# Attention's second key group one chunk pair earlier in the filler, three filler steps ahead of the first scores, one gate unit fetched at a fixed place

## The chip, the core and the metric

One Trainium2 core of one chip. A launch works on one sequence of 1024 positions (1040 with 16 meta tokens). The metric is device time in microseconds (us), median of several runs, lower is better. A profile is one further execution, recorded by the hardware profiler. Its engines are TensorE (PE, with its weight loads as PEld), VectorE (DVE), ScalarE (ACT), GpSimd (POOL) and SyncE (SP), which here only starts transfers. Each engine takes its instructions in the order of its own stream; what follows a waiting instruction waits with it.

## What is computed

Cut to what matters. `u` is the normalised input of 1040 rows and 1024 columns; one projection `w_in` feeds everything.

```python
z = u @ w_in
rq, rk, rv, rg, aq, ak, av, ag, gr, ga = _split_in(z)
# branch A: 4 heads of retention, forward and backward scans over 9 chunks of 128
o_r = _bidirectional_retention(rq, rk, rv, lg_f, lg_b)
o_r = groupnorm(o_r) * silu(rg);  y_r = o_r @ w_rb
# branch B: 8 query heads in 2 key groups, window of 128 to both sides, 16 meta keys, a sink
s_band = einsum(qb, kb) * scale;  s_meta = einsum(qb, km) * scale
m = maximum(max(s), sink);  p = exp(s - m)
p = p / (sum(p) + exp(sink - m))
o_a = p_band @ vb + p_meta @ vm
o_a = o_a * silu(ag);  y_a = o_a @ w_ab
mix = sigmoid(gr) * y_r + sigmoid(ga) * y_a
return h + rms_norm(mix @ w_o, post_w)
```

aq and ak get rotary positions. Inputs and output are float32.

## The kernel before

**Arithmetic.** Each float32 operand is split into a high and a low part of a shorter type. The high part is a cast (on ACT, or on POOL in `pool_hi`, L86), the low part the difference (`dve_lo`, L89, always on DVE). A product is three matmuls, high by high (L73), low by high (L74), high by low (L75), in `mm3` (L70 to L76). Names end in `h` and `l` for the two parts, so `aqh` and `aql` are the parts of the rotated query `aq`.

**Stages.** First the four retention heads, h = 0 to 3, in `retention`. Each runs forward over nine chunks (`stage1` makes the values `vh`, `vl`, the decayed keys and the scores, `stage2` the state) and then backward over chunks 8 to 1, where `pb` is the product of the query with the backward state (L601), DVE adds it into the chunk's output `op` (L602), and DVE splits the next state into `Shb`, `Slb`. Then the attention values (`gen_av`, tiles `pav`). Then attention: 32 chunks (hp, n), hp = 0 to 3 a pair of query heads, n = 0 to 7 a block of 128 positions. hp 0 and 1 use key group 0, hp 2 and 3 key group 1. Behind it come the four dense phases z, r, a and o (gates, two branch projections, the output projection), with seven products in place of eight for each pair of 2 x 2 blocks.

**One attention chunk.** `stage1(hp, n)`: for each of the two heads three score matmuls `ps`, DVE's masked minimum into `raw` (L1336), ACT's exponential into `p` with its sum in `den` (L1339); then DVE's reciprocal (L1342) and POOL's division (L1349). `stage2`: PE transposes `p` into `pt` (L1359, L1362, L1366), ACT and DVE split the result into `pah`, `pal`, `pm`, `pbh`, `pbl`. `stage3`: ten matmuls with the values into `po`. The driver loop at the end of `attention` puts, for chunk k: `stage1` of k+1, `stage2` of k, a number of filler steps, `stage3` of k-1. The tables `FILL[hp][n]` give the number of filler steps.

**Filler.** Attention alone would leave PE waiting for the softmax, so other matmul work is cut into steps, which generators hand out one at a time: `gen_aq(hp, i, es)` projects queries (tile `paq`, eight steps of three matmuls of 512 columns for each head and half of the positions, then `rope_evac` rotates the result on DVE and POOL), `gen_ak(g, pieces)` projects the keys of group g (tile `pak`, eight steps of three matmuls of 256 columns for each quarter), and `pre` makes two of the four column blocks of some gate units ahead (tiles `pe`; `pre_fetch` loads the unit's weights from memory into two buffers of the tag `wr`, `pre_sums` combines them in three DVE subtractions and additions, `pre_parts` splits the result). After each step the list `BEGUN` names what else is issued there: splitting of weights (`half_w`), of queries (`split_q`, `aqh` on ACT L646, `aql` on DVE), of a key quarter (`keys(g, i)`: `kTh` on ACT L692, `kTl` on DVE), fetches and sums for gate units, and rows of sums of the input (`sum_fetch`, `sum_row`). These are issued behind the last exponential, reciprocal and splits that were issued before them.

**What each engine's order follows from.** The order within an engine is the order of issue in the program, moved by a list scheduler; `tc.issue_after(x)` and `follow(...)` keep a block behind named instructions. In head 3 of retention the filler is `gen_ak(0)`, eight steps of `pre` (gate unit 6) and `gen_aq(0, 0)`; unit 6 is fetched and summed in `gen_pre` when its first step is reached in the program; nothing holds these sums, and the scheduler has moved them forward on DVE, to the seam between head 2's backward and head 3's forward loop. `raw` is one tile for each of the two heads of a pair, allocated at n = 0 of each pair in a pool that lies over memory of the retention stage, so a first writer waits for what read that memory, here the store of retention outputs (`ost`).

The functions below are those of the kernel before, with the line numbers of its profile; lines of the changed kernel lie 6 to 14 higher.

## Time and profile before

| | us |
|---|---|
| median of 3 runs | 1087.58 |
| lowest and highest of them | 1086.63, 1088.8 |
| the profiled execution, its own time | 1089.63 |
| its span in the profile | 1087.8 |
| PE busy | 1060.5 |
| DVE busy | 880.7 |
| ACT busy | 510.3 |
| POOL busy | 201.8 |

The profile gives the busy time of each engine over the span. A row of its timeline reads: start, duration, engine, line, operation, output and input tiles, and in brackets how long the engine had been idle before and what released it. A row of a window reads: the stretch, its length, busy time and count of PE, PEld, DVE, ACT and POOL, then the clock that PE was granted (1.00 is full speed), the share of the transfer engines and GB/s. Median of the runs and profiled execution differ by 1089.63 - 1087.58 = 2.05 us.

### The profile page before, as it was taken

Reading aid. Unit: us, or ns where it says so; the run is one execution under the profiler, and the core shown is the slowest. Engines: PE = TensorE matmul, PEld = TensorE weight load, DVE = VectorE, ACT = ScalarE, POOL = GpSimd, SP = SyncE. Lnnn points to the kernel's source line nnn. Section 1 sums busy time; section 2 is a strip of 40 time slices with the busy share of each in tenths; the row PEclk is TensorE's granted clock in tenths of the full one; section 3 lists DMA queues with packets and bytes.
Section 4 is the critical chain, followed back from the end, with each engine's and each line's share of the span. In section 5 each row is a group of like instructions: output and inputs, shape, how many; then the busy total and the mean of one; then the engine's idle time right before and its main releaser. Section 6 shows DMA issues by size and latency. Waiting matters only on the chain.

```text
span 1087.8 us, 17211 instructions
## 1 busy us (share of the span) xinstructions
PE 1060.5 (97%) x5939; PEld 915.7 (84%) x5939; DVE 880.7 (81%) x1805; ACT 510.3 (47%) x1126; POOL 201.8 (19%) x268
## 2 busy tenths in 40 slices
PE   8999999999999999989999999999999999999997
PEld 7898999988988788978888888887888888787886
DVE  7897778868976687787977988999789899767765
ACT  7241432512513465665567655545556546333442
POOL 3334225243332222332210000000000000110032
PEclk9999999999999999998999999999999999999999
DMA  7121102113121145342447788899944656789464
GB/s 289 39 69 58 47 34 69 58 49 98 50 78 59 49 147 170 120 155 88 164 143 241 263 263 289 269 345 346 377 164 146 218 198 206 231 204 331 121 116 79
DMA packets 88152, 175.19 MB, mean 161 GB/s; under 512 B 8912, under 2 KB 30928, under 8 KB 87248
## 3 DMA queue, kind: packets, MB, share of 16 engines
q1 hardware_dynamic: 84176, 167.51, 45.7%
q0 software_dynamic: 3456, 6.29, 4.0%
q8 instruction: 47, 0.77, 0.3%
q14 instruction: 41, 0.34, 0.1%
q10 hardware_dynamic: 432, 0.28, 0.1%
HBM read 119.52 MB, written 57.67 MB: 163 GB/s over the span
## 4 chain that ended last, share of the span: by engine, by line
PE 85%; DVE 6%; DMA 3%; issue 2%; ACT 2%; POOL 1%; SPq 0%; DVEq 0%; ACTq 0%; POOLq 0%
PE bz L73 8%; PE bz L74 8%; PE bz L75 8%; PE pv L73 3%; PE pv L74 2%; PE pv L75 2%; PE br L74 2%; PE br L73 2%; PE br L75 2%; PE bo L74 2%; PE bo L73 2%; PE bo L75 2%; PE ba L74 2%; PE ba L73 2%; PE ba L75 2%
## 5 line engine op out<-in xcount | busy, mean ns | idle before, releaser
L1196 POOL DMA_DIRECT2D mx_d<-c1a x4 | 3.7, 917 | 402.6 <-DVE c1a L1187 402.6
L74 PE MATMUL bz<-T,llz 128*128 128x512 f32 x192 | 75.7, 394 | 0.0
L75 PE MATMUL bz<-T,lhz 128*128 128x512 f32 x192 | 75.6, 395 | 0.0
L73 PE MATMUL bz<-T,lhz 128*128 128x512 f32 x192 | 75.2, 394 | 0.0
L73 PE MATMUL pv<-wh,big 128*128 128x256 f32 x256 | 73.2, 286 | 1.2 <-DVE m_qk L185 1.2
L74 PE MATMUL pv<-wh,big 128*128 128x256 f32 x256 | 73.0, 285 | 0.0
L75 PE MATMUL pv<-wl,big 128*128 128x256 f32 x256 | 72.7, 284 | 0.0
L73 PE MATMUL bz<-big,lhz 128*128 128x512 f32 x176 | 69.0, 395 | 0.8 <-ACT lhz L895 0.8
L74 PE MATMUL bz<-big,llz 128*128 128x512 f32 x176 | 69.7, 396 | 0.0
L75 PE MATMUL bz<-big,lhz 128*128 128x512 f32 x176 | 69.3, 394 | 0.0
L1339 ACT ACTIVATE p<-raw,nm 128x401 f32<-128x401 f32 (+1 forms) x64 | 38.4, 601 | 39.9 <-DVE nm L1336 39.7
L73 PE MATMUL paq<-big,wh 128*128 128x512 f32 x128 | 52.6, 411 | 0.0
L74 PE MATMUL paq<-big,wl 128*128 128x512 f32 x128 | 51.2, 400 | 0.0
L1349 POOL TENSOR_SCALAR p<-p,den 128x400 f32<-128x400 f32 (+1 forms) x60 | 33.8, 576 | 93.5 <-DVE den L1342 86.2
L75 PE MATMUL paq<-big,wh 128*128 128x512 f32 x128 | 50.8, 397 | 0.0
L73 PEld LDWEIGHTS pv<-wh,big 128*128 128x128 f32 x256 | 48.2, 188 | 1.7 <-DVE m_qk L185 1.5
L74 PEld LDWEIGHTS pv<-wh,big 128*128 128x128 f32 x256 | 48.2, 188 | 0.2
L75 PEld LDWEIGHTS pv<-wl,big 128*128 128x128 f32 x256 | 48.3, 189 | 0.0
L74 PEld LDWEIGHTS bz<-T,llz 128*128 128x128 f32 x192 | 36.2, 188 | 8.4
L75 PEld LDWEIGHTS bz<-T,lhz 128*128 128x128 f32 x192 | 36.2, 188 | 8.4
L73 PEld LDWEIGHTS bz<-T,lhz 128*128 128x128 f32 x192 | 36.2, 188 | 8.4
L1336 DVE CUSTOM_DVE_ANT_0 raw<-ps,mask,nsink 128x400 f32<-128x400 f32 (+1 forms) x64 | 36.6, 598 | 6.0 <-PE ps L75 5.5
(630 smaller groups left out, 3633.6 us busy)
## 6 DMA issues: line engine op xcount, KB each, us to landing
wrz<-in_w_in_dram SPq DMA_DIRECT2D x32, 512.0 KB, 6.2
wr<-in_w_in_dram SPq DMA_DIRECT2D x29, 512.0 KB, 3.9
e<-e SPq DMA_DIRECT2D x40, 256.0 KB, 4.2
we<-in_w_in_dram SPq DMA_DIRECT2D x16, 512.0 KB, 4.0
tg<-tg_d SPq DMA_DIRECT2D x32, 256.0 KB, 4.9
T<-preT SPq DMA_DIRECT2D x6, 1024.0 KB, 8.0
oTr_d<-ost SPq DMA_DIRECT2D x16, 256.0 KB, 2.1
xs<-in_xT_dram SPq DMA_DIRECT2D x16, 256.0 KB, 2.9
```

Source lines behind the costliest of these rows:

```text
L73: nc.tensor.matmul(o, ah, bh, start=first, stop=False, **kw)
L74: nc.tensor.matmul(o, al, bh, start=False, stop=False, **kw)
L75: latest[:] = [nc.tensor.matmul(o, ah, bl, start=False, stop=last, **kw).ins]
L1196: nc.gpsimd.dma_start(d, to, accum_op=ALU.add)
L1336: nc.vector.tensor_tensor_reduce(raw[e_][:, 1:1 + wid], s[:, 0:wid], mask[:, mo:mo + wid], -SCALE, nsink[:, hd:hd + 1], ALU.add, ALU.min, ...
L1339: last["exp"] = nc.scalar.activation(p[:, 0:1 + wid], raw[e_][:, 0:1 + wid], AF.Exp, scale=-1.0, bias=nm_[:, e_:e_ + 1], accum_out=den[:, ...
L1349: nc.gpsimd.tensor_scalar(pt[e_][:, 0:wid], pt[e_][:, 0:wid], den[:, e_:e_ + 1], 1.0, op0=ALU.mult, op1=ALU.mult)
```

## The change

It moves work and adds none: every matmul, split, load and store of before is there, in another order. Three places:

- **Head 3 of retention.** The loads of the key weights and of gate unit 6 are called at the forward loop's chunk 1, and the three sums of unit 6 at chunk 2, behind that chunk's latest `vl`. `gen_pre` leaves both out where they have been made.
- **Start of attention.** The two `raw` tiles are allocated at the start for the first pair. Three filler steps (`gen_aq(0, 1)`) stand in front of the first scores; the first chunk's filler is 3 steps fewer, and FILL's first two entries go from 8, 8 to 7, 9.
- **Second key group.** In the list of filler work, `gen_aq(2, 1)` is cut into its two heads, and the third and fourth quarters of the keys of group 1 stand behind one head each. The entries of `BEGUN` follow: the third quarter's split from step 122 to 115, the fourth's from 131 to 130, the second's from 100 to 102, the last query pair's weight splits from 115 and 119 to 121 and 125, and most later entries by one to nine steps.

```diff
-FILL = (8, 8, 7, 7, 7, 7, 7, 7), (7,) * 8, (7, 6, 6, 6, 6, 6, 6, 5), (5, 5, 5, 5, 5, 5, 8)
+FILL = (7, 9, 7, 7, 7, 7, 7, 7), (7,) * 8, (7, 6, 6, 6, 6, 6, 6, 5), (5, 5, 5, 5, 5, 5, 8)
...
+            if h == NH - 1 and c == 1:
+                wak.append(load_w(w_in, U_AK))
+                pre_fetch(6)
+            if h == NH - 1 and c == 2:
+                with tc.issue_after(state["vl"]):
+                    pre_sums(6)
...
         if u not in parts:
-            pre_fetch(u)
-            pre_sums(u)
+            if u not in fetched_w:
+                pre_fetch(u)
+                pre_sums(u)
             pre_parts(u)
...
-        oa, raw = [None], {}
+        oa = [None]
+        raw = [aw.tile([P, 401], F32, tag=f"raw{e_}", bufs=1, name=f"raw{e_}") for e_ in range(2)]
...
                 if n == 0:
-                    raw[e_] = aw.tile([P, 401], F32, tag=f"raw{e_}", bufs=1, name=f"raw{hd}")
+                    if hp:
+                        raw[e_] = aw.tile([P, 401], F32, tag=f"raw{e_}", bufs=1, name=f"raw{hd}")
...
-        fill = filler([hooked([gen_aq(0, 1), gen_aq(1, 0), pieces(pre, 8), gen_aq(1, 1), pieces(pre, 8), gen_aq(2, 0),
-                               gen_ak(1, (0, 1)), gen_aq(2, 1), gen_ak(1, (2, 3)), gen_aq(3, 0), gen_aq(3, 1), pre], BEGUN)])[0]
+        works = [gen_aq(0, 1), gen_aq(1, 0), pieces(pre, 8), gen_aq(1, 1), pieces(pre, 8), gen_aq(2, 0),
+                 gen_ak(1, (0, 1)), gen_aq(2, 1, (0,)), gen_ak(1, (2,)), gen_aq(2, 1, (1,)), gen_ak(1, (3,)),
+                 gen_aq(3, 0), gen_aq(3, 1), pre]
+        fill = filler([hooked(works, BEGUN)])[0]
...
+        with follow(*latest):
+            fill(3)
         with follow(*latest):
             stage1(0, 0)
...
-                    fill(FILL[hp][n])
+                    fill(FILL[hp][n] - 3)
...
-             63: [(sum_row, 2)], 66: [(sum_fetch, 3)], 70: [(half_w, 'k', 1, 0)], 73: [(half_w, 'k', 1, 1)],
-             76: [(split_q, 2, 0, 0)], 79: [(sum_row, 3)], 82: [(sum_fetch, 4)], 84: [(split_q, 2, 1, 0)],
-             93: [(sum_row, 4)], 95: [(sum_fetch, 5)], 100: [(keys, 1, 1)], 106: [(sum_row, 5), (fetch_aq, 3)],
-             108: [(split_q, 2, 0, 1)], 109: [(sum_fetch, 6)], 115: [(half_w, 'q', 3, 0)], 116: [(split_q, 2, 1, 1)],
-             119: [(half_w, 'q', 3, 1)], 122: [(keys, 1, 2)], 124: [(sum_row, 6)], 126: [(pre_fetch, 9)],
-             128: [(sum_fetch, 7)], 131: [(keys, 1, 3)], 136: [(pre_sums, 9)], 139: [(pre_parts, 9)],
...
+             63: [(sum_row, 2)], 67: [(sum_fetch, 3)], 70: [(half_w, 'k', 1, 0)], 73: [(half_w, 'k', 1, 1)],
+             76: [(split_q, 2, 0, 0)], 79: [(sum_row, 3)], 83: [(sum_fetch, 4)], 84: [(split_q, 2, 1, 0)],
+             94: [(sum_row, 4)], 97: [(sum_fetch, 5)], 102: [(keys, 1, 1)], 106: [(fetch_aq, 3)],
+             108: [(split_q, 2, 0, 1)], 110: [(sum_row, 5)], 115: [(keys, 1, 2)], 117: [(sum_fetch, 6)],
+             121: [(half_w, 'q', 3, 0)], 123: [(split_q, 2, 1, 1)], 125: [(half_w, 'q', 3, 1)],
+             128: [(pre_fetch, 9)], 130: [(keys, 1, 3)], 133: [(sum_row, 6)], 135: [(sum_fetch, 7)],
+             137: [(pre_sums, 9)], 140: [(pre_parts, 9)], 141: [(pre_fetch, 10)], 142: [(split_q, 3, 0, 0)],
```

**What moves, 1: DVE in head 3, at the seam between its backward loop of head 2 and the forward loop of head 3.** `we_1` is gate unit 6, `op_5` and `Slb_5` belong to the backward chunks of head 2, `vl_1` to forward chunk 1 of head 3. Before:

```order
L610 TENSOR_SCALAR op_7_2599<-op_7_2599,mv_8_3196,rs_8_3197 128x256
L772 TENSOR_TENSOR we_1_4520<-we_0_4519,we_1_4520 128x4x128
L89 TENSOR_TENSOR vl_1_3702<-pv_1_3676,vh_1_3701 128x256
L602 SCALAR_TENSOR_TENSOR op_5_2597<-pb_6_3271,qd,op_5_2597 128x256
L89 TENSOR_TENSOR Slb_5_3324<-Sb_5_3321,Shb_5_3323 128x256
L773 TENSOR_TENSOR we_1_4520<-we_1_4520,we_0_4519 128x4x128
L606 BN_STATS bs_6_3276<-op_5_2597 128x6
```

In the changed kernel the same place on DVE reads:

```order
L616 TENSOR_SCALAR op_7_2599<-op_7_2599,mv_8_3196,rs_8_3197 128x256
L89 TENSOR_TENSOR vl_1_3702<-pv_1_3676,vh_1_3701 128x256
L608 SCALAR_TENSOR_TENSOR op_5_2597<-pb_6_3271,qd,op_5_2597 128x256
L89 TENSOR_TENSOR Slb_5_3324<-Sb_5_3321,Shb_5_3323 128x256
L612 BN_STATS bs_6_3276<-op_5_2597 128x6
```

and the three sums stand two forward chunks later on DVE, 18 or 19 rows behind their old places:

```order
L89 TENSOR_TENSOR vl_3_3847<-pv_3_3821,vh_3_3846 128x256
L778 TENSOR_TENSOR we_1_3799<-we_0_3798,we_1_3799 128x4x128
L410 TENSOR_TENSOR cr<-cr,rbc 128x272
L410 TENSOR_TENSOR sr<-sr,rbc 128x272
L608 SCALAR_TENSOR_TENSOR op_3_2595<-pb_4_3383,qd,op_3_2595 128x256
L89 TENSOR_TENSOR Slb_3_3436<-Sb_3_3433,Shb_3_3435 128x256
L779 TENSOR_TENSOR we_1_3799<-we_1_3799,we_0_3798 128x4x128
```

The first sum no longer stands in front of `vl_1`, `op_5` and `Slb_5`.

**What moves, 2: PE at the first scores.** `pav` is the last tile of the values, `ps` the scores of chunk (0, 0) for the two heads, `paq_10` the filler. Before:

```order
L74 MATMUL pav_4941<-wh_1_4725,big_1_112 128x256
L75 MATMUL pav_4941<-wl_1_4726,big_0_110 128x256
L73 MATMUL ps_0_4974<-kTh_4311,aqh_00_4970 128x272
L73 MATMUL ps_0_4987<-kTh_4311,aqh_01_4983 128x272
L74 MATMUL ps_0_4974<-kTh_4311,aql_00_4971 128x272
L75 MATMUL ps_0_4974<-kTl_4312,aqh_00_4970 128x272
```

On PE in the changed kernel nine `paq_10` matmuls stand behind the last `pav`, of which the last three are shown, with the scores behind them:

```order
L73 MATMUL paq_10_4970<-big_0_109,wh_0_4591 128x512
L74 MATMUL paq_10_4970<-big_0_109,wl_0_4592 128x512
L75 MATMUL paq_10_4970<-big_1_111,wh_0_4591 128x512
L73 MATMUL ps_0_4990<-kTh_4318,aqh_00_4986 128x272
L73 MATMUL ps_0_5002<-kTh_4318,aqh_01_4998 128x272
L74 MATMUL ps_0_4990<-kTh_4318,aql_00_4987 128x272
L75 MATMUL ps_0_4990<-kTl_4319,aqh_00_4986 128x272
```

The order of the scores among themselves is the same. A little later on DVE, behind the second chunk's reciprocal `den_1`, the rotation of the filler's query tile (`m_aq_10`) stood ahead of the split of the first transposes (`pal_0`). Before:

```order
L1342 RECIPROCAL den_1_5000<-den_1_5000 128x2
L183 TENSOR_TENSOR m_aq_10_5048<-paq_10_5018,cr 128x512
L184 TENSOR_TENSOR m_aq_10_5049<-paq_10_5018,sr 64x512
L185 TENSOR_TENSOR m_aq_10_5049<-paq_10_5018,sr 64x512
L89 TENSOR_TENSOR pal_0_5063<-pt_0_0_5054,pah_0_5062 128x512
L89 TENSOR_TENSOR pm_4712<-pt_0_0_5059,pm_4712 16x256
```

The same place on DVE in the changed kernel:

```order
L1351 RECIPROCAL den_1_5014<-den_1_5014 128x2
L89 TENSOR_TENSOR pal_0_5053<-pt_0_0_5044,pah_0_5052 128x512
L89 TENSOR_TENSOR pm_4712<-pt_0_0_5049,pm_4712 16x256
L1345 ISA raw_4717,nm_2_5059<-ps_2_5061,mask,nsink 128x400
L1345 ISA nm_2_5059 128x1
L1345 ISA raw_4718,nm_2_5059<-ps_2_5068,mask,nsink 128x400
L1345 ISA nm_2_5059 128x1
L183 TENSOR_TENSOR m_aq_10_5103<-paq_10_4970,cr 128x512
```

`pal_0` now stands first, and the rotation behind the scores of the third chunk.

**What moves, 3: ACT and DVE around the third key quarter of group 1, in chunks (2, 1) to (2, 3).** The exponentials `p_2` are chunk (2, 2)'s, `akr_2` is the rotated third quarter, `kTh` the high part of the keys. On ACT before:

```order
L1398 COPY oa_6_6451<-po_7_6528 128x2x128
L1339 ACTIVATE p_2_6544,den_2_6539<-raw_6371,nm_2_6538 128x401
L1339 ACTIVATE p_2_6551,den_2_6539<-raw_6380,nm_2_6538 128x401
L1370 CAST pah_1_6567<-pt_2_1_6557 128x512
L1373 CAST pm_4713<-pt_2_1_6562 16x256
L1374 CAST pm_4713<-pt_2_1_6562 16x256
L1398 COPY oa_0_6618<-po_0_6610 128x2x128
L1382 CAST pbh_1_6574<-pt_2_1_6562 128x256
L692 CAST kTh_6276<-akr_2_6513 128x256
```

On ACT in the changed kernel the quarter's cast stands ahead of those exponentials:

```order
L1379 CAST pah_0_6476<-pt_2_0_6468 128x512
L1382 CAST pm_4712<-pt_2_0_6473 16x256
L1383 CAST pm_4712<-pt_2_0_6473 16x256
L698 CAST kTh_6276<-akr_2_6422 128x256
L1407 COPY oa_6_6447<-po_7_6518 128x2x128
L1348 ACTIVATE p_2_6534,den_2_6529<-raw_6363,nm_2_6528 128x401
```

On DVE before, the low parts of the last query pair's weights (`wl_0`, `wl_1`) and of a query half (`aql_11`) stood around chunk (2, 2)'s `raw`:

```order
L185 TENSOR_TENSOR m_ak_2_6515<-pak_2_6433,sr 64x256
L89 TENSOR_TENSOR wl_0_6494<-wr_0_6348,wh_0_6493 128x1024
L89 TENSOR_TENSOR aql_11_6501<-aq_11_6426,aqh_11_6500 128x512
L1336 ISA raw_6371,nm_2_6538<-ps_2_6540,mask,nsink 128x400
L1336 ISA nm_2_6538 128x1
L1336 ISA raw_6380,nm_2_6538<-ps_2_6547,mask,nsink 128x400
L1336 ISA nm_2_6538 128x1
L89 TENSOR_TENSOR wl_1_6521<-wr_1_6349,wh_1_6520 128x1024
```

On DVE in the changed kernel they stand one chunk later, behind the `raw` of chunk (2, 3):

```order
L1345 ISA raw_6372,nm_3_6609<-ps_3_6618,mask,nsink 128x400
L1345 ISA nm_3_6609 128x1
L89 TENSOR_TENSOR wl_0_6572<-wr_0_6340,wh_0_6571 128x1024
L89 TENSOR_TENSOR aql_11_6582<-aq_11_6507,aqh_11_6581 128x512
L183 TENSOR_TENSOR m_ak_3_6653<-pak_3_6514,cr 128x256
L184 TENSOR_TENSOR m_ak_3_6654<-pak_3_6514,sr 64x256
L185 TENSOR_TENSOR m_ak_3_6654<-pak_3_6514,sr 64x256
L89 TENSOR_TENSOR wl_1_6592<-wr_1_6341,wh_1_6591 128x1024
L1351 RECIPROCAL den_3_6610<-den_3_6610 128x2
```

The first query tile of the last pair, `paq3_00`, is begun at the same filler step, 128, in both kernels, and reads `wl_0` from its first step and `wl_1` from its fifth.

19 lines of the change are left out of this document (9 added, 10 removed).

## The prediction

> **What bounds the kernel now.** First the page: busy time, and the chain that ended last.
>
> ```profile
> PE 1060.5 (97%) x5939; PEld 915.7 (84%) x5939; DVE 880.7 (81%) x1805; ACT 510.3 (47%) x1126; POOL 201.8 (19%) x268
> PE 85%; DVE 6%; DMA 3%; issue 2%; ACT 2%; POOL 1%; SPq 0%; DVEq 0%; ACTq 0%; POOLq 0%
> ```
>
> PE is busy for 1060.5 of 1087.8 us. The change moves matmuls and takes none away, so it can only gain where PE stands still, 27.3 us in all, or where its matmuls run longer than elsewhere. So the second view is PE's waits, by what was waited for, with total, count and longest.
>
> ```profile
> PE ps L73 <- ACT kTh L692: 4.3, 1, 4.3
> PE pt L1359 <- DVE pal L89: 1.9, 2, 1.2
> ...
> PE pb L73 <- DVE op L602: 1.4, 1, 1.4
> PE ps L74 <- DVE aql L89: 1.4, 2, 1.2
> ...
> PE ps L73 <- ACT aqh L646: 1.1, 1, 1.1
> ```
>
> These five rows, 10.1 us, are the places that the change touches. The third view is PE's granted clock in windows: behind the columns for PE, PEld, DVE, ACT and POOL stands the clock.
>
> ```profile
> 250.00:253.00 3.00, 1.62 (x15) 1.44 (x13) 1.60 (x4) 0.90 (x3) 0.00 (x0) 1.00 0.06 20
> 351.00:353.00 2.00, 2.00 (x8) 1.78 (x9) 1.31 (x6) 1.17 (x5) 0.46 (x1) 0.73 0.03 7
> 353.00:355.00 2.00, 2.00 (x6) 1.55 (x5) 0.68 (x3) 1.33 (x4) 0.89 (x3) 0.50 0.00 0
> 355.00:356.00 1.00, 1.00 (x5) 0.84 (x4) 0.00 (x0) 0.00 (x0) 0.79 (x2) 0.83 0.00 0
> 490.00:492.00 2.00, 1.90 (x6) 1.90 (x7) 0.96 (x3) 1.28 (x3) 0.00 (x0) 0.50 0.48 195
> 492.00:494.00 2.00, 2.00 (x11) 1.74 (x10) 1.83 (x6) 0.92 (x3) 0.00 (x0) 0.50 0.17 68
> 494.00:496.00 2.00, 2.00 (x9) 1.78 (x9) 1.16 (x4) 1.61 (x5) 0.00 (x0) 0.68 0.40 135
> 680.00:760.00 80.00, 79.22 (x341) 63.65 (x340) 75.59 (x125) 42.02 (x73) 0.00 (x0) 1.00 0.94 320
> ```
>
> Behind the waits at 346 to 350 and at 486 to 490 PE ran at half its clock for some microseconds. Those matmuls count as busy, so the waits' rows don't show this loss. Against full clock it is 2 x 0.27 + 2 x 0.50 + 1 x 0.17 = 1.71 us at the first place and 2 x 0.50 + 2 x 0.50 + 2 x 0.32 = 2.64 at the second. At 250 to 253 the clock stayed at 1.00.
>
> **Part A, gate unit 6's sums in head 3.** The timeline of DVE, then of PE:
>
> ```profile
> 251.40 0.69 DVE L772 TENSOR_TENSOR we<-we,we 128x512 f32<-128x512 f32 x1 [2.74 <-DMA we<-in_w_in_dram]
> 252.34 0.48 DVE L602 SCALAR_TENSOR_TENSOR op<-pb,qd,op 128x256 f32<-128x256 f32 x1
> 252.97 0.36 PE L73 MATMUL pb<-Shb,qh 128*128 128x256 f32 x1 [1.38 <-DVE op L602]
> ```
>
> DVE stood 2.74 us at the first sum, waiting for the unit's load, and `vl`, `op` and `Slb` stood behind it. PE's `pb` needs the bank that `op` reads, and waited 1.38. In the changed order the sums stand two chunks later. The loads keep their place in SP's queue, so nothing is fetched later; DVE reaches `op` about 2.7 us sooner, before PE asks. I take the whole 1.38. The new place has no trace: if one of the three sums (0.69) delays PE there, 0.69 is left; if the other two also stop holding back what they stood in front of, one such length comes on top. Bounds 0.7 and 2.1.
>
> **Part B, the first scores.** PE's, DVE's and POOL's rows:
>
> ```profile
> 347.75 0.91 PE L73 MATMUL ps<-kTh,aqh 128*128 128x272 f32 x2 [1.07 <-ACT aqh L646]
> 349.84 0.39 PE L74 MATMUL ps<-kTh,aql 128*128 128x272 f32 x1 [1.19 <-DVE aql L89]
> 350.44 0.40 PE L74 MATMUL ps<-kTh,aql 128*128 128x272 f32 x1
> 362.53 0.63 PE L1359 MATMUL pt<-ident,p 128*128 128x128 f32 x4 [1.24 <-DVE pal L89]
> ...
> 347.71 0.55 DVE L1281 MEMSET pm<- 128x256 f32 x2
> 348.98 0.21 DVE L1334 COPY raw<-nsink 128x1 f32<-128x1 f32 x2 [0.72 <-DMA oTr_d<-ost]
> 349.11 1.28 DVE L89 TENSOR_TENSOR aql<-aq,aqh 128x512 fp32r<-128x512 f32 x2
> 359.56 0.69 DVE L183 TENSOR_TENSOR m_aq<-paq,cr 128x512 f32<-128x512 f32 x1 [5.04 <-PE paq L75]
> 361.69 0.69 DVE L89 TENSOR_TENSOR pal<-pt,pah 128x512 fp32r<-128x512 f32 x1
> ...
> 352.54 0.97 POOL L1349 TENSOR_SCALAR p<-p,den 128x272 f32<-128x272 f32 x2 [9.84 <-DVE den L1342]
> ```
>
> A filler step's length comes from two rows of one kind, 15 starts apart:
>
> ```profile
> 355.63 0.39 PE L75 MATMUL paq<-big,wh 128*128 128x512 f32 x1
> ...
> 359.13 0.39 PE L75 MATMUL paq<-big,wh 128*128 128x512 f32 x1
> ```
>
> 3.50 / 15 = 0.233 us for a matmul of 512 columns, 0.70 for a step of three. Three steps are 2.10 us of work that now runs while the splits `aqh` and `aql` are made. This is the first term: PE works from about 346.5 to 348.6 instead of standing. Next the splits themselves. `raw`'s first writes no longer wait 0.72 for the store of `ost`: they come at 347.71 + 0.55 = 348.26, the first `aql` ends near 349.1 and the second, 0.64 long, near 349.8, where its matmul stood at 350.44. That is 0.60. The store's memory now lies under the second `aql`, but DVE reaches that after 348.98, when the store is over. Third, PE's gaps shrink to some tenths each, so the clock's loss of 1.71 goes. Fourth, the three rotations `m_aq` (3 x 0.69) no longer stand before `pal`, whose lateness cost 1.24; I leave 0.2 of it. Sum B: 2.10 + 0.60 + 1.71 + 1.24 - 0.2 = 5.45.
>
> The price is fewer steps behind the scores. Four are left between the second chunk's scores and the first transposes, 2.8 us in place of 5.6. These hide the softmax of chunk (0, 0): its `p` is there at 352.54 + 0.97 = 353.5, and 0.6 sooner in the new order, 352.9, and the scores now end near 351.5. With 2.8 us PE comes to the transposes at 354.3, so 1.4 us are to spare. The cover is thinner but there. Bounds: 2.10 + 0.60 = 2.7, if neither the clock nor `pal` gives anything, and 2.10 + 1.19 + 1.71 + 1.24 = 6.2.
>
> The clock's rule is weighed here. The window of 250 to 253 has PE busy 1.62 of 3.00 and no drop follows; the waits of 1.07 and 1.19 are followed by 0.50 at 353 to 355. The Trainium skill, in "TensorE: Matmul & The Clock Gate", Part 1, gives half rate after at least one idle window of about 3.4 us. This trace agrees at 490, behind 4.31 us of idling, but shows a drop at 353 where no single wait was longer than 1.19. By that rule alone the drop at 353 would have another cause and stay; the time would then be 1.7 us longer.
>
> **Part C, the second group's third key quarter.**
>
> ```profile
> 481.57 0.83 PE L1359 MATMUL pt<-ident,p 128*128 128x128 f32 x4 [0.70 <-DVE pal L89]
> ...
> 482.59 0.36 PE L73 MATMUL pak<-big,wh 128*128 128x256 f32 x1
> ...
> 484.69 0.28 PE L75 MATMUL pak<-big,wh 128*128 128x256 f32 x1
> ...
> 490.10 0.70 PE L73 MATMUL ps<-kTh,aqh 128*128 128x400 f32 x1 [4.31 <-ACT kTh L692]
> ...
> 486.37 0.63 ACT L1339 ACTIVATE p<-raw,nm 128x401 f32<-128x401 f32 x1 [2.22 <-DVE nm L1336]
> 489.64 0.41 ACT L692 CAST kTh<-akr 128x256 fp32r<-128x256 f32 x1
> ...
> 482.77 0.43 DVE L185 TENSOR_TENSOR m_ak<-pak,sr 64x256 f32<-64x256 f32 x1
> 483.22 1.23 DVE L89 TENSOR_TENSOR wl<-wr,wh 128x1024 fp32r<-128x1024 f32 x1
> 484.37 1.23 DVE L89 TENSOR_TENSOR aql<-aq,aqh 128x512 fp32r<-128x512 f32 x1
> 485.63 0.64 DVE L1336 CUSTOM_DVE_ANT_0 raw<-ps,mask,nsink 128x400 f32<-128x400 f32 x1
> ```
>
> Chunk (2, 3) is the first that reads the third quarter. Its cast at 489.64 stood on ACT behind the exponentials of chunk (2, 2), which waited 2.22 for `raw`, and `raw` stood on DVE behind `wl` and `aql`. In the new order the quarter is projected eight steps sooner and cast ahead of those exponentials, and `wl` and `aql` stand behind `raw` of (2, 3). So 4.31 goes, with it the 2.64 of clock, and the 0.70 before `pt`, since a rotation of queries has moved away from the `raw` in front.
>
> A new wait comes. The query tile `paq3_00` still begins at step 128, and its `wl` halves are now split just before. I measure from the start of the last score matmul of chunk (2, 3). On PE follow its 400 columns (400/512 of 0.233, 0.18), the transposes (482.59 - 481.57 = 1.02), one `pak` step (484.69 - 482.59 over 17 starts is 0.124, so 0.37) and one matmul of 0.23: the first low weight is wanted at 1.80. On DVE: 0.39 until the scores are there (estimate from the 512-column row of part B), 0.64 for `raw`, 1.23 for `wl`: 2.26. PE waits 0.46. The second half is wanted four steps, 2.80, later; DVE needs `aql` (0.64 alone, as half of the 1.28 in part B, or 1.23 as above), three `m_ak` of 0.43 and 1.23: 3.16 to 3.75. That is 0.36 to 0.95. Together 0.8 to 1.4; I take 0.9, near the lower end, since 0.64 is what `aql` took with nothing beside it. Queued behind the second `wl` on DVE are the reciprocal of (2, 3) and `pal` of (2, 2); six score and ten value matmuls on PE lie before their readers. Sum C: 0.70 + 4.31 + 2.64 - 0.9 = 6.75. Bounds: 0, if the new wait is as long as the old, and 7.65 without a new one.
>
> Other moved entries (rows of sums, fetches of units 9 to 13, `keys` 1 and 3) cost nothing by my walk through the order, since their readers stand many steps off; a miss is the last rival below. **Sum:** 1.38 + 5.45 + 6.75 = 13.6. The profiled execution took 1089.63, so 1076.0 for one like it; that execution lies 2.05 above the median of the runs, 1087.58, so **1074.0**.
>
> **Rivals.** *The clock drops stay*, because smaller gaps at both places still trigger them: 1.71 + 2.64 = 4.35 come back, 1078.3. Against it speaks 250 to 253, with 1.38 of idling and clock 1.00; for it, that waits of only 1.07 and 1.19 sufficed at 347. *The keys' wait only changes its name*: `paq3_00` waits for `wl` about as long as the scores did for `kTh`, and C gives nothing: 1087.58 - 1.38 - 5.45 = 1080.8. For it speaks that DVE had `wl` and `aql` at 1.23 each, and both now stand one chunk nearer to their readers. *No change*: what is gained in attention is lost again in the dense phases, whose transfers would then set the end, or the moved waits come back elsewhere. 1087.6. Against it the window 680 to 760: transfers are busy 0.94 there, yet PE 79.22 of 80. *Slower*: five units (9 to 13) pass through two `wr` buffers, and their hooks come 1 to 2 steps later than before; if each load then misses its sums, PE waits for it at the unit's first step. Each miss priced as the keys' wait with its clock, 4.31 + 2.64 = 6.95, two cancel the gain (13.9 against 13.6), and three give 1087.58 - 13.6 + 20.85 = 1094.8. Against it: one step later is 0.7 us.
>
> **How the numbers follow.** Forecast as summed, 1072 to 1077: 0.60. Clock stays: 0.13. Keys' wait renamed: 0.14. No change: 0.07. Slower: 0.06. All high bounds at once give 16.0, 1071.6; the range goes from 1071 to 1082, a little over the second rival, and leaves out 0.13; all low bounds together (3.4, 1084.2) lie in that rest. A measurement of this kernel can tell about 0.2%, 2.2 us, from no change. The first three cases are faster by more than that, 0.87; same 0.07; slower 0.06.
>
> **What would show it.** In the changed kernel's waits the rows of `pb` on `op`, of `ps` on `kTh` and of `ps` on `aqh` are gone, and those on `pal` and `aql` are some tenths. The clock is 1.00 in every window around the first scores and around chunk (2, 3). A row of `paq` waiting for `wl` (and perhaps `wh`) is there, with about 0.9. Over 2 us in that row, or a clock below 0.8 behind it, makes C wrong; a new wait of `pt` for POOL's `p` behind the first scores makes B's cover wrong; a wait of `pe` for `weh` or `wel` in the last attention chunks is the slow case. PE's busy time should fall by about 4.35 and its idle time by about 9.3.

## The result and the profile after

| | before, us | after, us |
|---|---|---|
| median of the runs | 1088.19 (6 runs) | 1077.27 (6 runs) |
| lowest and highest | 1086.35, 1090.46 | 1076.72, 1078.95 |
| profiled execution, its own time | 1089.63 | 1077.22 |
| its span | 1087.8 | 1075.5 |

The ratio is 0.990, 95% interval 0.9884 to 0.9917: the changed kernel is faster by 10.9 us (9.0 to 12.6). The forecast was 1074.0 in a range of 1071 to 1082; the time is in the range, and the gain is smaller than the 13.6 that were summed. The two profiled executions differ by more than the medians, 12.4 us.

First the changed kernel's page, busy time and chain:

```profile
PE 1054.8 (98%) x5939; PEld 911.2 (85%) x5939; DVE 880.6 (82%) x1805; ACT 509.7 (47%) x1126; POOL 201.6 (19%) x268
PE 83%; DVE 8%; ACT 3%; issue 2%; DMA 2%; SPq 0%; POOL 0%; DVEq 0%; POOLq 0%; ACTq 0%
```

PE's busy time fell by 1060.5 - 1054.8 = 5.7 us, the time at half clock among it, and its idle time from 27.3 to 1075.5 - 1054.8 = 20.7, by 6.6. Of these, 0.95 changed its column in the first 36.5 us, where nothing was altered: the profile of before has 30.59 busy and 5.91 idle there, the changed kernel 29.65 and 6.85, and a second profile of before (e4 below) 29.61 and 6.89. Without it busy fell by 4.8 and idle by 7.6. In the chain that ended last DVE's share rose from 6% to 8%. The next view, PE's waits (total, count, longest), says where:

```profile
PE pt L1371 <- DVE pbl L89: 1.3, 2, 1.0
...
PE paq L74 <- DVE wl L89: 1.0, 1, 1.0
PE pt L1371 <- DVE raw L1343: 0.8, 1, 0.8
...
PE ps L74 <- DVE aql L89: 0.7, 1, 0.7
...
PE pt L1368 <- DVE pal L89: 0.3, 1, 0.3
```

The rows of `pb` on `op`, of `ps` on `kTh` and of `ps` on `aqh` are gone, and `pal` is down from 1.9 to 0.3. But of the rows in attention that came or grew (`pbl`, `wl`, `raw`), only `wl` was forecast. They all name DVE, and so does the row of `aql`, which now stands at another place. The granted clock, in windows of the changed kernel around the first scores and around chunk (2, 3):

```profile
351.00:353.00 2.00, 2.00 (x13) 1.68 (x12) 0.17 (x1) 0.14 (x2) 1.18 (x2) 1.00 0.00 0
482.00:484.00 2.00, 1.33 (x6) 1.12 (x7) 1.97 (x5) 2.00 (x7) 0.00 (x0) 1.00 0.19 49
490.00:492.00 2.00, 2.00 (x10) 1.60 (x9) 1.31 (x4) 1.42 (x6) 1.18 (x2) 1.00 0.00 0
670.00:750.00 80.00, 80.00 (x345) 64.55 (x344) 75.64 (x125) 42.20 (x73) 0.00 (x0) 1.00 0.94 327
```

The clock column reads 1.00 in all of them, also around the new wait at 482. In the dense phase PE is busy 80.00 of 80 with transfers at 0.94, so no transfer took the place of what was saved.

**Where the time went.** A matmul that both kernels run once in every chunk is a mile post: the last value matmul of a chunk. Before:

```profile
369.71 0.28 PE L1393 MATMUL po<-pm,vm 80*128 80x256 f32 x1
...
594.23 0.28 PE L1393 MATMUL po<-pm,vm 80*128 80x256 f32 x1
```

and in the changed kernel:

```profile
362.27 0.28 PE L1402 MATMUL po<-pm,vm 80*128 80x256 f32 x1
...
583.52 0.28 PE L1402 MATMUL po<-pm,vm 80*128 80x256 f32 x1
```

The first row of each kernel is chunk (0, 0), the second the last chunk, (3, 7). Their differences, with the chunks between where the lead changes, and ahead of them one transpose (L489) in head 3 of retention:

| mile post | before | after | lead | change of the lead |
|---|---|---|---|---|
| a transpose in retention, head 3 | 280.12 | 278.09 | 2.03 | +2.03, part A |
| (0, 0) | 369.71 | 362.27 | 7.44 | +5.41, part B |
| (0, 2) | 386.21 | 379.38 | 6.83 | -0.61 |
| (2, 0) | 485.51 | 478.57 | 6.94 | +0.11 |
| (2, 1) | 499.45 | 487.35 | 12.10 | +5.16, with the row above part C: 5.27 |
| (2, 4) | 521.43 | 509.85 | 11.58 | -0.52 |
| (2, 7) | 541.65 | 529.74 | 11.91 | +0.33 |
| (3, 1) | 554.55 | 543.85 | 10.70 | -1.21 |
| (3, 7) | 594.23 | 583.52 | 10.71 | +0.01 |

In front of part A's place the two profiles stand within 0.06 us of each other. So A gave more than was forecast (2.03 for 1.38) and B as much (5.41 for 5.45); C gave 5.27 in place of 6.75, and behind it and at chunk (0, 2) a net 2.0 us were lost again (12.71 - 10.71). Three places that the prediction does not speak of account for most of this; the second of them lies within part C. The dense phases run alike; the profiled executions end 12.3 apart mainly because the one of before has two waits there that the one of the changed kernel has not:

```profile
PE bz L73 <- ACT lhz L895: 0.8, 1, 0.8
...
PE bo L73 <- ACT lho L895: 0.5, 1, 0.5
```

They come and go: a second profile of the changed kernel (e7 below) has 0.9 for `lhz`, a third (e11) none.

**The three places.** The first is the scores of chunk (0, 4), here in the changed kernel, DVE's rows, then PE's:

```profile
370.77 0.68 DVE L778 TENSOR_TENSOR we<-we,we 128x512 f32<-128x512 f32 x1
371.37 0.69 DVE L89 TENSOR_TENSOR aql<-aq,aqh 128x512 fp32r<-128x512 f32 x1
...
372.11 0.45 PE L74 MATMUL ps<-kTh,aql 128*128 128x400 f32 x1 [0.69 <-DVE aql L89]
```

Before, the same rows of DVE's `aql` and of PE read:

```profile
378.17 0.69 DVE L89 TENSOR_TENSOR aql<-aq,aqh 128x512 fp32r<-128x512 f32 x1
...
378.91 0.45 PE L74 MATMUL ps<-kTh,aql 128*128 128x400 f32 x1 [0.17 <-DVE aql L89]
```

DVE's order is the same in both: a sum of gate unit 7 stands ahead of `aql`. PE comes 7.4 us sooner and DVE's `aql` only 378.91 - 372.11 = 6.8, and the rest is a wait.

The second is chunk (1, 7)'s transposes, in the changed kernel:

```profile
455.40 0.43 DVE L736 TENSOR_TENSOR xs<-xs,xs 128x256 f32<-128x256 f32 x1 [1.78 <-ACT xs L732]
...
459.39 0.69 DVE L183 TENSOR_TENSOR m_aq<-paq,cr 128x512 f32<-128x512 f32 x1
...
461.51 0.42 DVE L89 TENSOR_TENSOR pbl<-pt,pbh 128x256 fp32r<-128x256 f32 x1
461.86 0.20 DVE L1343 COPY raw<-nsink 128x1 f32<-128x1 f32 x2
...
462.09 0.38 PE L1371 MATMUL pt<-ident,p 128*16 128x128 f32 x2 [0.80 <-DVE raw L1343]
```

DVE stood 1.78 at a row of input sums (`xs`), whose rows come from memory and through ACT, and what follows in its queue came late: the rotation, `pbl`, `raw`. It stood in the same place before, for 1.68, and PE did not notice:

```profile
462.12 0.43 DVE L730 TENSOR_TENSOR xs<-xs,xs 128x256 f32<-128x256 f32 x1 [1.68 <-ACT xs L726]
```

What changed is PE's cover: the filler hands out steps by count, and of the steps in front of these transposes three are now `pak` steps in place of `paq` steps. With the prediction's lengths, 0.37 and 0.70, that is 3 x 0.33 = 1.0 us less work between. (PE's row names `raw`, which follows `pbl` directly.)

The third is chunk (3, 2)'s transposes, in the changed kernel:

```profile
537.17 1.23 DVE L89 TENSOR_TENSOR wel<-we,weh 128x1024 fp32r<-128x1024 f32 x1 [0.58 <-ACT weh L787]
538.32 0.42 DVE L89 TENSOR_TENSOR pbl<-pt,pbh 128x256 fp32r<-128x256 f32 x1
...
538.88 0.38 PE L1371 MATMUL pt<-ident,p 128*16 128x128 f32 x2 [0.98 <-DVE pbl L89]
```

`wel` is the low part of gate unit 11's weights. Its hook, `pre_parts`, went from step 164 to 165, and with that `wel` came to stand in front of chunk (3, 1)'s `pbl` on DVE, 0.58 of waiting for ACT and 1.23 of work. Before, it stood a chunk earlier, ahead of the `raw` of (3, 2), and that `pbl` came behind it with `wel` long done:

```profile
543.18 1.22 DVE L89 TENSOR_TENSOR wel<-we,weh 128x1024 fp32r<-128x1024 f32 x1 [0.74 <-ACT weh L781]
544.32 0.63 DVE L1336 CUSTOM_DVE_ANT_0 raw<-ps,mask,nsink 128x400 f32<-128x400 f32 x1
...
548.95 0.42 DVE L89 TENSOR_TENSOR pbl<-pt,pbh 128x256 fp32r<-128x256 f32 x1 [0.44 <-ACT pbh L1382]
```

### The profile page after: what moved, and what is told of

It reads as the page before. It is cut to its first block, busy times and chain, and to the rows that moved or that the text cites. A ratio compares the mean times of both kernels' runs of the same rounds, so it can differ in the third digit from the quotient of the medians.

```text
span 1075.5 us, 17218 instructions
## 1 busy us (share of the span) xinstructions
PE 1054.8 (98%) x5939; PEld 911.2 (85%) x5939; DVE 880.6 (82%) x1805; ACT 509.7 (47%) x1126; POOL 201.6 (19%) x268
## 4 chain that ended last, share of the span: by engine, by line
PE 83%; DVE 8%; ACT 3%; issue 2%; DMA 2%; SPq 0%; POOL 0%; DVEq 0%; POOLq 0%; ACTq 0%
PE bz L74 8%; PE bz L75 8%; PE bz L73 8%; PE pv L73 3%; PE pv L74 3%; PE pv L75 3%; PE br L74 2%; PE br L73 2%; PE br L75 2%; PE bo L73 2%; PE bo L74 2%; PE bo L75 2%; PE ba L74 2%; PE ba L73 2%; PE ba L75 2%
## 5 line engine op out<-in xcount | busy, mean ns | idle before, releaser
L589 ACT ACTIVATE ost<-to,rnw 128x128 f32<-128x128 f32 x64 | 20.0, 364 | 46.0 <-PE to L584 38.7
```

The costliest lines, as they stand in the source:

```text
L589: nc.scalar.activation(ost[0][:, e_, w0:w0 + P], to[:, P * e_:P * e_ + P], AF.Copy, scale=rnw[:, 2 * h + e_:2 * h + e_ + 1])
```

## The experiments

The first four kernels ran on one chip, with 28 executions of before between them (median 1089.07): each part alone, and before once more. The edits are cut to the lines that matter; `...` stands for the rest.

**e1, part A alone.** The edit is the diff's lines in `retention` and `gen_pre`.

```diff
+            if h == NH - 1 and c == 1:
+                wak.append(load_w(w_in, U_AK))
+                pre_fetch(6)
+            if h == NH - 1 and c == 2:
+                with tc.issue_after(state["vl"]):
+                    pre_sums(6)
...
```

> The kernel before with the change's first part alone (fetch and sums of gate unit 6 in head 3 of retention). Theory, that each part takes its own wait off PE's path and nothing takes it back: PE's wait of pb for op (1.38 us) is gone, the last transposes of the retention stage come 1.4 to 2.0 us sooner than in the kernel before, and the time falls by as much, 0.13 to 0.19%. Rival, that later stages swallow a head start: the wait goes, and the end comes where it came before, within 0.5 us.

Measured: 1086.35 (12 runs), ratio 0.998, interval 0.9969 to 0.9992, so 2.7 us less (0.9 to 3.4), a little over the 1.4 to 2.0 expected. The wait of `pb` is gone; the mile post of retention stands 2.15 sooner, near the 2.03 of the whole change. A is worth 2.0 to 2.7.

**e2, part B alone.**

```diff
-FILL = (8, 8, 7, 7, 7, 7, 7, 7), (7,) * 8, (7, 6, 6, 6, 6, 6, 6, 5), (5, 5, 5, 5, 5, 5, 8)
+FILL = (7, 9, 7, 7, 7, 7, 7, 7), (7,) * 8, (7, 6, 6, 6, 6, 6, 6, 5), (5, 5, 5, 5, 5, 5, 8)
...
+        raw = [aw.tile([P, 401], F32, tag=f"raw{e_}", bufs=1, name=f"raw{e_}") for e_ in range(2)]
...
+        with follow(*latest):
+            fill(3)
...
-                    fill(FILL[hp][n])
+                    fill(FILL[hp][n] - 3)
```

> The kernel before with the second part alone (three filler steps ahead of the first scores, raw allocated at the start, FILL 7, 9). Theory: PE's waits of ps for aqh and aql shrink from 2.26 us to about 0.5, the granted clock stays 1.00 in the microseconds behind them, and a wait of ps for aql in chunk (0, 4) of about 0.7 us appears, because DVE is still behind while PE has gained: 4.6 to 5.5 us less, 0.42 to 0.5%. Rival, that the drop of the clock at 353 has another cause than the two short waits: the clock falls to 0.50 behind the first scores here as well, and only 3 to 4 us are gained.

Measured: 1083.29 (6 runs), ratio 0.9954 (0.9937 to 0.997), 5.8 us less (3.3 to 6.9), where 4.6 to 5.5 were expected. The wait for `aqh` is gone and the clock behind the first scores is whole:

```profile
352.00:354.00 2.00, 2.00 (x10) 1.64 (x9) 0.63 (x3) 1.22 (x4) 1.47 (x3) 1.00 0.00 0
```

The new wait of 0.69 at chunk (0, 4) is here too, so it belongs to B and not to the moved steps of C. The 4.3 for `kTh` stay.

**e3, part C alone.** The edit is the order of `works` and the whole of `BEGUN`, of which one line each is shown.

```diff
...
-                               gen_ak(1, (0, 1)), gen_aq(2, 1), gen_ak(1, (2, 3)), gen_aq(3, 0), gen_aq(3, 1), pre], BEGUN)])[0]
+                 gen_ak(1, (0, 1)), gen_aq(2, 1, (0,)), gen_ak(1, (2,)), gen_aq(2, 1, (1,)), gen_ak(1, (3,)),
...
```

> The kernel before with the third part alone (key quarters of group 1 in the new order, BEGUN's entries moved). Theory: the wait of ps for kTh (4.31 us) and the low clock behind it are gone, the waits at the first scores and the low clock at 353 stay; new waits: paq for wl about 1.0 us, pt for raw about 0.8 at chunk (2, 0), pt for pbl about 1.0 at (3, 2). Net 3.9 to 5.5 us less than before, 0.36 to 0.5%. Rival, that the keys' wait only changes its name: the sum of PE's new waits reaches the 4.3 us of the old one and less than 2 us are gained.

Measured: 1085.35 (11 runs), ratio 0.9969 (0.9957 to 0.9981), 3.7 us less (2.1 to 4.7), just under the 3.9 to 5.5 expected. The 4.31 for `kTh` and the dip behind it are gone, the low clock at the first scores is still there, 0.50 from 352 to 354. In place of `kTh` this kernel's waits have:

```profile
PE pt L1362 <- DVE pbl L89: 1.3, 2, 1.0
...
PE paq L74 <- DVE wl L89: 1.0, 1, 1.0
...
PE pt L1362 <- DVE raw L1334: 0.6, 1, 0.6
```

So the second and the third place are there with C alone, and with them C is worth about 4 us (3.7 by the runs) and not the forecast 6.75. The three parts alone add to 2.7 + 5.8 + 3.7 = 12.2, about what they give together.

**e4, before once more**, with no edit.

> The kernel before, unchanged, to see how its executions differ among themselves. Theory, that the low clock behind the two waits comes in some executions and not in others: the executions spread over 3 to 4 us, and the longer ones have the lower mean granted clock (0.994 to 0.996 against 0.998 or more). Rival: the spread has nothing to do with the clock, and all executions show the same mean clock to 0.001.

Measured: 1088.92 (12 runs), ratio 1.0 (0.9989 to 1.0012). Its profile has the same waits at the first scores (1.07, 1.19 and 1.24) as the first profile of before, but another clock behind them:

```profile
350.00:352.00 2.00, 2.00 (x7) 1.58 (x8) 1.29 (x5) 0.86 (x3) 0.00 (x0) 0.50 0.10 29
352.00:354.00 2.00, 2.00 (x7) 1.91 (x6) 1.24 (x4) 1.07 (x4) 0.97 (x2) 0.50 0.00 0
354.00:356.00 2.00, 2.00 (x6) 1.54 (x6) 0.37 (x3) 0.72 (x2) 0.74 (x2) 0.50 0.00 0
356.00:358.00 2.00, 2.00 (x10) 1.65 (x9) 0.00 (x0) 0.00 (x0) 0.43 (x1) 0.97 0.00 0
```

Half clock from 350 to 356 loses 3 x 2 x 0.50 + 2 x 0.03 = 3.1 us; in the first profile it was 1.71. The clock term of a forecast from one execution is thus known to one or two us only. The theory, that some executions have the low clock and others not, did not come out in that form: the 12 executions have mean clocks of 0.990 to 0.995, and none reached 0.998; what differs is how much of it each has.

**e5 and e6, the two halves of B.** e5 has only the early `raw` tiles, e6 only the three filler steps with `FILL` 7, 9.

```diff
+        raw = [aw.tile([P, 401], F32, tag=f"raw{e_}", bufs=1, name=f"raw{e_}") for e_ in range(2)]
```

> The kernel before with raw allocated at the start, and nothing else. Theory, that the two halves of the second part act separately: DVE's write of raw no longer waits for the store of ost, the second head's aql matmul comes 0.6 us sooner, PE's wait for aqh (1.07 us) and the lateness of pal (1.24) stay: 0.6 us of PE's idle time less, and the clock still drops behind the waits. Rival, that raw's place is what the whole second part is worth: the waits at the first scores fall below 1 us in all and 3 us or more are gained.

Measured: 1087.35 (10 runs), ratio 0.9983 (0.9972 to 0.9994), 1.4 us less of 1088.77. The first wait for `aql` falls from 1.19 to 0.32; those for `aqh` (1.07) and `pal` (1.25) stay, and so does the low clock.

```diff
+        with follow(*latest):
+            fill(3)
...
-                    fill(FILL[hp][n])
+                    fill(FILL[hp][n] - 3)
```

> The kernel before with the three filler steps ahead of the first scores and FILL 7, 9, but raw allocated as before. Theory: 2.1 us of work move into the wait; PE still waits about 1.2 us for aql, since raw's write still waits for the store of ost (or the store now ends ahead of it, and the wait is below 0.5); pal is on time. 3.3 to 5 us of PE's time less up to the end of chunk (0, 1). Rival, that the steps are no use without raw: the wait for aql grows by what the steps fill, and less than 1.5 us are gained.

Measured: 1083.88 (4 runs), ratio 0.9949 (0.9934 to 0.9965), 4.9 us less. The wait for `aqh` is gone, the one for `aql` stays at 0.79, `pal` is 0.28, and the clock is whole:

```profile
352.00:354.00 2.00, 2.00 (x11) 1.74 (x11) 1.26 (x5) 1.56 (x5) 0.92 (x2) 1.00 0.00 0
```

The three steps carry most of B: they take the idle time, `pal` and the clock together. With `raw` alone one wait shrinks and the clock still drops.

**e7, the changed kernel again, and e8, four mends in it.** e7 ran beside e5, e6 and e8.

> The changed kernel once more, beside runs of the kernel before on this chip. Theory, that the parts add up: e1 to e3 measured 2.7, 5.8 and 3.7 us against 1089.07, together 12.2, so the changed kernel is 11 to 13 us faster here, with mean clocks of 0.997 or more. Rival, that the parts overlap: under 10 us.

Measured: 1079.42 (5 runs), ratio 0.9898 (0.9881 to 0.9915). The ratio gives 11.1 us less (9.3 to 13.0), the two medians lie only 9.35 apart (1088.77 before); so this run does not settle whether the parts add up in full or overlap by a microsecond or two. The waits are at the same places: 0.69 for `aql`, 0.69 for `raw`, 0.97 for `wl`, 0.33 and 0.98 for `pbl`.

e8 tries to remove the new waits: one step of `FILL` moves from chunk (1, 5) to (1, 6), unit 7's hooks come later, `wl` is held right behind the `raw` of chunk (2, 2), a chunk ahead of its place in the changed kernel, and units 10 and 11 go back to the steps of before. Of `BEGUN` only the entries that move are shown, here and below, and the arguments that carry `last["raw"]` to the split are left out.

```diff
-FILL = (7, 9, 7, 7, 7, 7, 7, 7), (7,) * 8, (7, 6, 6, 6, 6, 6, 6, 5), (5, 5, 5, 5, 5, 5, 8)
+FILL = (7, 9, 7, 7, 7, 7, 7, 7), (7, 7, 7, 7, 7, 6, 8, 7), (7, 6, 6, 6, 6, 6, 6, 5), (5, 5, 5, 5, 5, 5, 8)
...
-    22: [(pre_sums, 7)], 25: [(pre_parts, 7)], 26: [(pre_fetch, 8)]
+    24: [(pre_sums, 7)], 26: [(pre_parts, 7)], 27: [(pre_fetch, 8)]
-    121: [(half_w, 'q', 3, 0)]
+    if chunks[k + 1] == (2, 2):
+        half_w('q', 3, 0, last["raw"])
-    151: [(pre_sums, 10)], 153: [(pre_parts, 10)], 154: [(pre_fetch, 11)], 162: [(pre_sums, 11)], 165: [(pre_parts, 11)], 166: [(pre_fetch, 12)]
+    149: [(pre_sums, 10)], 152: [(pre_parts, 10)], 153: [(pre_fetch, 11)], 161: [(pre_sums, 11)], 164: [(pre_parts, 11)], 165: [(pre_fetch, 12)]
```

> The changed kernel with four edits against its new waits: unit 7's sums two steps later (behind aql of chunk (0, 4)); FILL of hp 1 7, 7, 7, 7, 7, 6, 8, 7 (one long step more in front of chunk (2, 0)); wl of the last query pair's first half on DVE between raw and the reciprocal of chunk (2, 2); units 10 and 11 back at the steps of before. Theory: the waits ps for aql 0.7, pt for raw 0.8, paq for wl 1.0 (and 0.2 behind it), pt for pbl 1.0 go or shrink to 0.2 each: 2.5 to 3.5 us less than the changed kernel, the last value matmul of attention near 580.3 us in place of 583.5. Rival, that DVE is the bound in these chunks and the waits only move on: under 1 us less.

Measured: 1081.23 (5 runs), ratio 0.9917 (0.9902 to 0.9932), not better than the changed kernel. The expected 2.5 to 3.5 us did not come. By the mile posts against the changed kernel, the `FILL` mend gained 0.96 and the `wl` mend 1.79; unit 7's lost more than it gained (`pe` then waits 1.01 for its `wel`), and 4.80 went at chunk (2, 6). There this kernel has, on DVE and on PE:

```profile
510.61 0.69 DVE L779 TENSOR_TENSOR we<-we,we 128x512 f32<-128x512 f32 x1 [1.71 <-DMA we<-in_w_in_dram]
```

```profile
519.02 0.41 PE L1369 MATMUL pt<-ident,p 128*128 128x128 f32 x2 [3.25 <-POOL p L1359]
```

Unit 10's load had not landed when DVE came to its sums; DVE stood, the `raw` behind it came late, and PE waited 3.25 for the softmax. Behind that wait PE ran at half clock from 519.6 to 523.0, which makes most of the rest of the 4.80.

**e9, e10 and e11 part these mends**, on one chip. e9 keeps `FILL` and `wl` and has unit 11's hooks one step sooner; e10 is the changed kernel with only unit 10's hooks as before; e11 is the changed kernel.

```diff
-    162: [(pre_sums, 11)], 165: [(pre_parts, 11)]
+    161: [(pre_sums, 11)], 164: [(pre_parts, 11)]
```

> The changed kernel with the mends that helped by place in e8 and without those that cost: FILL of hp 1 7, 7, 7, 7, 7, 6, 8, 7; wl of the last query pair's first half between raw and the reciprocal of chunk (2, 2); of units 9 to 13 only unit 11 one step sooner; unit 7 as in the changed kernel. Theory: the value matmuls come 1.0 us sooner from chunk (1, 7) on, 1.8 more from (2, 1) on and 1.1 more from (3, 1) on: 3.9 us in all, the last one near 579.6 in an execution like that of the changed kernel (583.5), and 3 to 4.5 us (0.3 to 0.4%) less time. Rival, as in e8: a transfer or DVE is the bound there, another wait takes their place, and under 1.5 us are left.

```diff
-    151: [(pre_sums, 10)], 153: [(pre_parts, 10)]
+    149: [(pre_sums, 10)], 152: [(pre_parts, 10)]
```

> The changed kernel with unit 10's sums and splits alone two steps and one step sooner, at the steps of the kernel before. Theory, that e8 lost its 4.8 us at chunk (2, 6) here: DVE waits at a sum for the unit's load (1.7 us in e8) with raw of chunk (2, 7) behind it, and PE then waits 3 us or more for p; the value matmuls from (2, 6) on are 3 to 5 us later than in the changed kernel. Rival, that it was the earlier wl or the FILL of hp 1 that brought chunk (2, 6) ahead of the load: no loss above 1 us at (2, 6).

> The changed kernel on the chip of e9, for the comparison with it. Theory: 1.0 to 1.2% faster than the kernel before, and the sites of its waits as in the two profiles so far, each within 0.15 us. Rival: the new waits differ from execution to execution as the clock does.

Measured: e9 1077.2 (4 runs), ratio 0.9897 (0.9878 to 0.9916); e11 1077.58 (4 runs), 0.9903 (0.9888 to 0.9918); so no difference between them, and e9's 3 to 4.5 us did not come. In e11 the waits stand at the same places, but not all within the 0.15 expected: the one at the second place is 0.39, where it was 0.80 and 0.69. e9 gained 1.73 at chunk (2, 1) and lost 1.86 at (3, 0), where unit 11's sums, one step sooner, met their load:

```profile
529.82 0.89 DVE L779 TENSOR_TENSOR we<-we,we 128x512 f32<-128x512 f32 x1 [0.99 <-DMA we<-in_w_in_dram]
```

e10 ran once, 1080.9, so its time says little by itself; its trace lost 5.29 at chunk (2, 6) alone, by the same chain as e8, some 3.4 of it PE's wait for `p` and 1.7 half clock behind it (0.50 from 523.0 to 526.3):

```profile
513.15 0.69 DVE L778 TENSOR_TENSOR we<-we,we 128x512 f32<-128x512 f32 x1 [1.83 <-DMA we<-in_w_in_dram]
```

So the later hooks of unit 10 in the change are no side effect: sums at the old step are too early for the load. That PE is ahead is not enough to explain it, since the load is issued sooner by as much, at 506.26 in place of 517.58. But it took 6.9 us to land, where it took 4.7 before, and 6.7 in the changed kernel and in e8. Why it takes longer there was not tried.

**e12, three orders altered again.** `FILL` and `wl` as in e9, unit 11's sums left at 162, and its `pre_parts` later instead of sooner.

```diff
-    165: [(pre_parts, 11)], 166: [(pre_fetch, 12)]
+    167: [(pre_parts, 11)], 166: [(pre_fetch, 12)]
```

> The changed kernel with three orders altered: the filler steps of group 1 become 7, 7, 7, 7, 7, 6, 8, 7; the first query weights of group 3 (wl) are split on DVE right behind the raw of chunk (2, 3), and not before; unit 11's pre_parts stands at step 167 in place of 165, its sums stay at 162. Theory (waits that the moves created on DVE are what the change lost): against the changed kernel the wait of pt for raw in front of chunk (2, 0) falls (0.5 to 1.0 us gained), paq no longer waits 0.97 for wl (gained at chunk (2, 1), up to 1.8), and pt no longer waits 0.98 for pbl, since pbl then stands ahead of wel on DVE (1.0 gained at chunk (3, 1)); together 2 to 3.5 us, about 1074.5 beside 1077.4 for the changed kernel. First rival (each of these gains ends at the next place where DVE is late, as in the run before it, where 1.86 came back at unit 11): within 1 us of the changed kernel, with a new wait of 1 us or more behind step 162. Second rival (pre_parts now stands behind pre_fetch(12), and pe asks for the weights of unit 11 too soon): pe waits 1 us or more for wel, slower than the changed kernel by 0.5 to 2 us.

Measured: 1074.6 (4 runs; 1073.69 to 1075.44), ratio 0.9864 (0.9848 to 0.9881), 14.7 us less than the 1089.3 of before beside it. In the edit as in the trace `wl` stands behind the `raw` of chunk (2, 2), not of (2, 3) as the expectation has it. By the ratios to before, each on its own chip, this version beats both kernels: its interval lies below that of the changed kernel as it ran first (0.9884 to 0.9917) and as e11 (0.9888 to 0.9918), and touches that of e7 (0.9881 to 0.9915). Against e11 the lead grows by 1.78 at chunk (2, 1) and by 1.14 at (3, 1), with no loss behind them. The order on DVE at the third place is now:

```profile
534.65 0.42 DVE L89 TENSOR_TENSOR pbl<-pt,pbh 128x256 fp32r<-128x256 f32 x1 [0.44 <-ACT pbh L1392]
...
536.10 1.22 DVE L89 TENSOR_TENSOR wel<-we,weh 128x1024 fp32r<-128x1024 f32 x1
```

and of the new waits this kernel has left:

```profile
PE ps L74 <- DVE aql L89: 0.9, 2, 0.7
...
PE pt L1372 <- DVE pbl L89: 0.3, 1, 0.3
```

The theory held for the second and the third place and for `wl`: these waits can be had back by order alone. The 0.7 for `aql` at chunk (0, 4) stays.

**The second place across the runs.** It shows best how DVE's wait for a load becomes PE's. The left column is the idle time of DVE at that `xs` row, the right one PE's wait at chunk (1, 7)'s transposes, both from the profile of the run:

| kernel | filler in front | DVE's wait | PE's wait |
|---|---|---|---|
| before, first profile | `paq` only | 1.68 | none |
| e4 | `paq` only | 1.43 | none |
| e2, e5, e6 | `paq` only | 1.29, 1.54, 1.79 | none |
| e1 | `paq` only | 2.56 | 0.58 |
| e11 | with `pak` | 1.37 | 0.39 |
| e3 | with `pak` | 1.58 | 0.63 |
| e7 | with `pak` | 1.62 | 0.69 |
| after | with `pak` | 1.78 | 0.80 |
| e10 | with `pak` | 1.94 | 1.00 |
| e12, e8, e9 | with `pak`, `FILL` mended | 0.46, 0.57, 0.88 | none |

With the new filler PE waits for what DVE's wait exceeds 0.93 to 0.98; with the old one, by e1 alone, for what exceeds 1.98, and there is none up to 1.79. The cover is thinner by 1.0, the 1.0 worked out above. e1 shows that the place was close to its limit before. With `FILL` mended DVE's own wait is short, so these three rows do not show how thick the cover is there.

## Why the prediction was right, and where it was short

**Part A, 1.38: under-sized.** Exactly this wait went, and the mechanism is as told. Its size is one execution's number: in e2 to e6, which keep it, it is 0.8 to 1.6. The lead is 2.03 in the trace and 2.7 (0.9 to 3.4) by the runs of e1. Of the 0.65 beyond, 0.21 is a wait of `pkv` for DVE's `rs` in the forward loop that is gone too; the rest lies in gaps too short to tell apart.

**Part B, 5.45: right, 5.41 in the trace, 5.8 by e2.** The steps fill the idle time, `pal` keeps 0.28 where 0.2 was left, and the thinner cover holds, as no wait for POOL's `p` came behind the first scores. Its clock term, 1.71, was one execution's number; e4 shows 3.1 for the same waits. The rule of the Trainium skill that was weighed there ("TensorE: Matmul & The Clock Gate", Part 1: half rate after an idle window of about 3.4 us) would by itself have kept the drop, since there was no idle stretch of that length; e2 and e6 show it gone with the waits. In before PE is busy for 0.93 + 0.69 = 1.62 of the 4 us ahead of it, with no wait over 1.19, and that was enough:

```profile
346.00:348.00 2.00, 0.93 (x7) 0.66 (x5) 0.77 (x3) 1.90 (x5) 0.00 (x0) 1.00 0.23 75
348.00:350.00 2.00, 0.69 (x3) 0.34 (x3) 1.28 (x5) 0.21 (x1) 0.00 (x0) 1.00 0.99 283
```

**Part C, 6.75: over-sized, 5.27 at chunk (2, 1), about 4 with what follows.** The 4.31, the 2.64 of clock and the 0.70 went; the forecast wait for `wl` came, with 0.96 where 0.9 was taken:

```profile
480.84 0.63 DVE L1345 CUSTOM_DVE_ANT_0 raw<-ps,mask,nsink 128x400 f32<-128x400 f32 x1
481.39 1.22 DVE L89 TENSOR_TENSOR wl<-wr,wh 128x1024 fp32r<-128x1024 f32 x1
...
482.67 0.50 PE L74 MATMUL paq<-big,wl 128*128 128x512 f32 x1 [0.96 <-DVE wl L89]
```

That the figure fits is luck in part. The sum had 0.46 for the first weight and 0.36 to 0.95 for the second; in the trace the first costs 0.96, since the first head's `raw`, behind a `pbl`, stands on DVE in front of the one that was counted, and the second under 0.2. The term that is missing is the second place, 0.80; some 0.6 more are in gaps too short for the list. Past the end of C another 0.2 went up to chunk (2, 7), with a new wait of 0.30 for `pbl` on the way, and 1.2 at the third place.

**The step that failed** is the sentence "Other moved entries ... cost nothing by my walk through the order, since their readers stand many steps off". It looked at the readers of what was moved, and not at what the moved work is now queued in front of on DVE: `wel` was in time for `pe`, but stood ahead of `pbl`. And it did not ask where steps of `pak` had come in place of steps of `paq`, 0.37 for 0.70 by the prediction's own lengths. The 0.6 at chunk (0, 4) has no moved entry at all; there B brings PE forward by more than DVE. Together these are 0.6 + 0.8 + 1.2 = 2.6 of the 2.9 by which the lead at the end of attention (10.7) misses 13.6; in the rest A's surplus of 0.65 stands against the small losses of C, 0.6 and 0.2. That errors of both signs partly cancel is luck, and so is part of how near the sum came.

**The rivals.** Clock drops stay: refuted, 1.00 in all windows of attention. Keys' wait changes its name: 0.96 of 4.31, so no. No change: refuted by the ratio. Slower by loads that miss their sums: it did not happen, but the mechanism is real, and e10 shows its price, 5.29 for one miss where 6.95 was set. It was argued from the wrong side, though: at unit 10 the hooks that come later are what avoids it.

**Busy and idle.** Busy fell by 5.7 (forecast 4.35) and idle by 6.6 (9.3), or by 4.8 and 7.6 without the 0.95 of the first 36.5 us. What idle time lacks of the forecast is in the main the new waits on DVE.

## What to carry to other kernels

When one engine is brought forward, look at every place where another engine was only just in time, in the order of that engine's own queue; the reader of the moved work is only one of those who may wait. Where cover is handed out by count, multiply each step by its length, since a step of half the length is half the cover. A load that was in time for an engine's old position must be checked again for the new one, and the consumer moved with it.
